# Attention maps turned by VectorE and a way through DRAM, and the products from z to the b branch in one fixed order

## The chip, the cores and the metric

The kernel runs on one core of a Trainium2 chip. The core has five engines with a queue of instructions each: TensorE (PE; its weight loads are shown apart as PEld) multiplies matrices into PSUM, VectorE (DVE) and ScalarE (ACT) work on rows of SBUF and PSUM, GpSimd (POOL) works on SBUF and issues DMAs, SyncE (SP) issues DMAs. An engine takes its instructions in the order of its queue; one that has to wait holds up everything behind it on that engine. Engines wait for one another through semaphores.

The metric is device microseconds (us) of one execution, lower is better. The kernel before takes 750.28 us, the median of 3 runs (750.06 to 750.52).

## The reference: what is computed

The program is an encoder of two layers over 256 tokens of 1024 features, all in float32. Each layer normalises its input, multiplies it by one wide matrix (`w_in`), and feeds two branches, which are gated, projected and added:

```
proj = h @ w_in[l]
(q_a, k_a, v_a, ab_a, z_a, q_b, k_b, v_b, z_b,
 gate_a, gate_b) = jnp.split(proj, SPLIT_IDX, axis=-1)
y_a = gated_delta_branch(q_a, k_a, v_a, ab_a, z_a, ...)
y_b = diff_attention_branch(q_b, k_b, v_b, z_b, cos, sin, ...)
merged = (jax.nn.sigmoid(gate_a) * (y_a @ w_pa[l])
          + jax.nn.sigmoid(gate_b) * (y_b @ w_pb[l]))
x = x + merged @ w_out[l]
```

The b branch is differential attention with 8 heads: of each head two softmax maps over 256 keys are made, one is taken from the other, and the difference is multiplied by the head's values:

```
s = jnp.einsum('nbhqd,nbhkd->nbhqk', q_blk, k)
p = jax.nn.softmax(s, axis=-1)
a = p[0] - lam * p[1]
return jnp.einsum('bhqk,bhkd->bhqd', a, v)
```

The a branch is a gated delta rule over chunks. Its triangular solve is done here by substitution within blocks of 32 tokens (on DVE), whose results are then merged on TensorE to 64 and 128.

## The kernel before

Tokens lie on the partitions in two tiles of 128. A projection of 512 columns (`proj_tm`) walks the 1024 features in eight steps of 128; a step has six products of 512 columns, for the two token tiles times three terms, since each float32 operand is split into a high and a low part (ACT casts the high part, L308, DVE subtracts for the low part, L310). A weight chunk of 512 KB, loaded by SP, serves two steps. The steps from the projections `zb` (two), `za` (two), `gb` (two), `ga` (two) to `pb` (two) are numbered 0 to 79 in what follows: step 8 is the first of the second `zb` projection, step 32 the first of `gb`.

Between these products lie the small ones of attention and of the delta rule. For a head h:

- `scores` (L1053) makes four products `sc` on TensorE, then on DVE two row maxima `mx` (L1069), on ACT four exponentials into `es` (L1071) with their sums, and on DVE the factor `cc` (L1074, L1075) and the difference of the two maps, in `es[:, 0]` (L1077, two instructions).
- `turn` (L1081) turns the map with four TensorE transposes into the PSUM tile `at` (L1088) and copies it with ACT to SBUF, tile `aT` (L1090): keys on the partitions.
- `attend` (L1093) multiplies: `av`, four products of 128x128 (L1099; each is two instructions in the trace), with `aT` as the weights that are loaded into TensorE. ACT copies `av` out and sums squares.

In the kernel before, `place(n)` names the last product of step n, and `behind(...)` makes a small product come after that one in TensorE's queue. This is a lower bound. Within it a list scheduler of the framework, which goes by priorities and by its own estimate of when operands are ready, decides the place of each instruction in every queue, and it also moves the products of a projection against one another.

Beside this, DVE runs the 31 rounds of the substitution (L870, L871, tiles `fstmp` and `X`) from the q/k projections of attention to the end of `za`, and the transposes by 32x32 blocks of the delta rule's values (`turn_squares`, L135). Their blocks go through DRAM and back to land in their new places (`bounce`: one issue on POOL out, tile `bnc_v`, L140, and four issues back, tile `tb_v`, L142). After the last round, `spread_blocks` copies `X` turned into `lt` (L874) and issues four DMAs to DRAM on POOL (`udr`, L878). `merges` reads them back: `T` (L905, four issues; those of the second group on SP) and `U` (L909, four issues). The gated attention output goes the same way through DRAM (`send`, `fetch`: `bny_yb`, L251, and `zb`, L257).

Of the kernel before, what the change touches and what calls it, by code (L numbers as in the profile page):

```python
# [8 lines left out]
F32 = mybir.dt.float32  # L9
# [40 lines left out]
def hybrid_encoder(  # L50
# [53 lines left out]
    mark = {}  # L104
# [53 lines left out]
    def norm_row(w_row, nm):  # L158
# [14 lines left out]
        for i in range(3):  # L173
            mm = T.matmul(wb[i > 0], one if i else tri[:, 0, :], hl[:, i - 1] if i else row,
                          start=i < 2, stop=i != 1)
            tc.keep_in_program_order(mm)
# [138 lines left out]
    def proj_tm(act, w, c0, n, evac, nm, places=(None,) * 4, spare=(), later=None, turned=(), between=None,  # L315
                banks=None, held=None, first=(), raws={}):

        accs = (banks or banks2)(f"pp_{nm}")
        for kt, hi, lo in weights(w, c0, n, nm, places, later=later, spare=spare, turned=turned, held=held,
                                  first=first, raws=raws):  # L320
            for m in range(NM):
                ts_ = slice(m * P, (m + 1) * P)
                o = accs[m][:, :n]
                T.matmul(o, act[kt // 4][:, 0, kt % 4, ts_], hi, start=kt == 0, stop=False)  # L324
                T.matmul(o, act[kt // 4][:, 0, kt % 4, ts_], lo, start=False, stop=False)  # L325
                mark["proj"] = T.matmul(o, act[kt // 4][:, 1, kt % 4, ts_], hi, start=False,  # L326
                                        stop=kt == KT - 1).ins
                mark["done", nm, kt] = mark["proj"]
        if between:
            between()  # L330
        for m in range(NM):
            evac(m, accs[m][:, :n])
# [76 lines left out]
    for _ in range(5):  # L409
        mm = T.matmul(idle[:, :P], ones, ones, start=True, stop=True)  # L410
        tc.keep_in_program_order(mm)
# [22 lines left out]
    for m in range(NM):  # L434
        mm = T.matmul(pos_p[:, m : m + 1], pos_r[:, m * P : (m + 1) * P], ones[0:1, 0:1], start=True, stop=True)
        mark["pos"] = mm.ins
        tc.keep_in_program_order(mm)
# [69 lines left out]
    for l in range(DEPTH):  # L507
# [86 lines left out]
        def qk_part(s_, i):  # L594
                def evac_qk(m, ps):
# [11 lines left out]
                    for b in range(4):  # L607
# [4 lines left out]
                proj_tm(hT, wl, (C_QB, C_KB)[s_] + 512 * i, 512, evac_qk, f"qk{l}{s_}{i}",  # L612
                        turned=(0, 1) if (s_, i) == (0, 1) else ())
# [170 lines left out]
        def gram(nm, g, c, slot, after=None):  # L784
            gp = (bank if slot else bank_c)(f"{nm}{l}{g}{c}")
            for j4 in range(4):
                kqh = kq[:, 4 * g + j4, c]
                with behind(after):
                    mark[nm, g, c] = T.matmul(gp[:, j4 * P : (j4 + 1) * P], kqh[:, 0, :], kqh[:, slot, :],
                                              start=True, stop=True).ins  # L790
# [35 lines left out]
        def weigh_q(g, c, after):  # L826
            bv = B[:, c, 4 * g : 4 * g + 4]
            with tc.high_priority(offset=HP):
                gp = gram("kq", g, c, 1, after)
# [67 lines left out]
        def merges(g):  # L897
# [18 lines left out]
            order = [(c, j4, mm, d) for c, j4 in every for mm in range(2) for d in range(2)]  # L916
            order.sort(key=lambda k: k != (0, 0, 1, 1))
            first = mark["pin"]
            for n_, (c, j4, mm, d) in enumerate(order):
                b0, b1 = srcdst(d, mm)  # L920
                co = 32 * (b0 % 2)
                with behind(first):
                    mm_ = T.matmul(y64p[blk(b1), c, j4, :], A[blk(b0), g, c, j4, blk(b1)],
                                   T64[blk(b0), tix(d, c, j4), co : co + 32], start=True, stop=True)
                if n_ == 0:
                    first = mm_.ins
            S.copy(y64, y64p)
            yield
            first = mark["pin"]
            zt64 = v4(bank_c(f"zt64{l}{g}")[:, :256])  # L930
            z64 = v4(bank_c(f"z64{l}{g}")[:, :256])
            for c, j4 in every:
                for mm in range(2):
                    for d in range(2):
                        b0, b1 = srcdst(d, mm)
                        with behind(first):
                            T.matmul(zt64[blk(b0), c, j4, :], y64[blk(b1), c, j4, :],
                                     U[blk(b1), tix(d, c, j4), blk(b1)], start=True, stop=True)
            for c, j4 in every:
                for d in range(2):  # L940
                    b0, b1 = srcdst(d, d)
                    T.matmul(z64[blk(b1), c, j4, :], U[blk(b1), tix(d, c, j4), blk(b1)],
                             y64[blk(b1), c, j4, :], start=True, stop=True)
            for d in range(2):
                td = slice(8 * d, 8 * d + 8)
                fl = lambda z, b: z[blk(b)].rearrange("p c h i -> p (c h) i")
                for mm in range(2):
                    b0, b1 = srcdst(d, mm)
# [7 lines left out]
            for c, j4 in every:  # L956
                for d in range(2):
                    ha, hb = halves[d], halves[1 - d]
                    with behind(mark["pin"]):
                        T.matmul(y128p[hb, c, j4, :], A[ha, g, c, j4, hb], T64[ha, tix(d, c, j4), :],  # L960
                                 start=True, stop=True)
# [3 lines left out]
            for c, j4 in every:  # L965
                for d in range(2):
                    ha, hb = halves[d], halves[1 - d]
                    with behind(mark["pin"]):
                        T.matmul(zt128[ha, c, j4, :], y128[hb, c, j4, :], U[hb, tix(d, c, j4), hb],
                                 start=True, stop=True)  # L970
# [5 lines left out]
        def chunks(g):  # L976
# [5 lines left out]
            def four(nm, lhs, rhs):  # L982
                ps = (bank if g else bank_c)(f"{nm}{l}{g}")
                for j4 in range(4):
                    with behind(mark["pin"]):
                        T.matmul(ps[:, j4 * P : (j4 + 1) * P], lhs(j4), rhs(j4), start=True, stop=True)
# [32 lines left out]
            for c in range(NM):  # L1019
                po = (bank if g else bank_c)(f"po{l}{g}{c}")  # L1020
                for j4 in range(4):
                    for d in range(2):
                        yy = y1[d] if d == c else y2[d]
                        with behind(mark["pin"]):
                            T.matmul(po[:, j4 * P : (j4 + 1) * P], B[:, c, h0 + j4, d, :], yy[:, j4, :],
                                     start=d == 0, stop=d == 1)
# [26 lines left out]
        def scores(h, after):  # L1053
# [3 lines left out]
            for qt in range(NM):  # L1057
                for n in (1, 0):
                    rows = slice(64 * n, 64 * n + 64)
                    with behind(None if qt or not n else after), tc.high_priority(offset=HP):  # L1060
                        mm = T.matmul(sp[n][:, qt * SEQ : (qt + 1) * SEQ],  # L1061
                                      qkT[h // 4][rows, 0, h % 4, qt * P : (qt + 1) * P],
                                      qkT[h // 4][rows, 1, h % 4, :], start=True, stop=True)
                    mark["sc", h] = mm.ins
                    if qt or not n:
                        tc.keep_in_program_order(mm)
# [14 lines left out]
        def turn(h, es, at):  # L1081
            with tc.high_priority(offset=HP):
                ap_ = bank(f"at{l}{h}")
                aT = work.tile([P, NM, SEQ], F32, tag="w2a", name=f"aT{l}{h}", bufs=2)
                for qt in range(NM):
                    for kt in range(NM):
                        with behind(at):
                            mark["at", h] = T.transpose(ap_[:, kt * SEQ + qt * P : kt * SEQ + (qt + 1) * P],  # L1088
                                                        es[:, 0, qt, kt * P : (kt + 1) * P], ident).ins
                S.copy(aT.rearrange("p k q -> p (k q)"), ap_)  # L1090
            return aT

        def attend(h, aT, after):  # L1093
            with tc.high_priority(offset=HP):
                op_ = bank(f"av{l}{h}")
                for qt in range(NM):
                    for kt in range(NM):
                        with behind(after):
                            T.matmul(op_[:, qt * P : (qt + 1) * P], aT[:, kt, qt * P : (qt + 1) * P],  # L1099
# [284 lines left out]
```

## Time and profile before

| what | value |
|---|---|
| median of 3 runs | 750.28 us (750.06 to 750.52) |
| span of the profiled execution, first to last instruction | 748.5 us |
| what lies around the span, by the median | 1.8 us |
| PE busy | 739.3 us, 99% of the span |
| DVE busy | 586.5 us, 78% |
| ACT busy | 481.2 us, 64% |
| POOL busy | 139.5 us, 19% |
| DMA | 135.46 MB, mean 181 GB/s |
| granted TensorE clock, mean | 0.998 |

The profiled execution is known by its span alone; its own time is that span and the 1.8 us that the runs have around it.

Each row of a profile names a line of the kernel, an engine, an operation and the tiles as out<-in. In a group's row `x128 | 18.2, 274` means 128 instructions, 18.2 us in which at least one of them ran, and 274 ns as the mean length of one. Matmuls overlap one another, so what one costs is read from the starts in the timeline, not from its length. A row of the timeline begins with its start and its length in us, and may merge several instructions (x8).

### The profile page before, as it was taken

The numbers are of one execution on the slowest core, as the hardware profiler recorded it, in microseconds if no ns is written. First come the engines' busy times: TensorE is split into PE (matmuls) and PEld (weight loads), VectorE is DVE, ScalarE is ACT, GpSimd is POOL, SyncE is SP. The second block draws the span as 40 slices with busy tenths as digits, with TensorE's granted clock in tenths as the row PEclk, the third lists the DMA queues.
The fourth block names the chain that finished last, engine by engine and source line by source line (L and its number), as shares of the span: only waits on it lengthen the run. The fifth ranks groups of instructions, "written<-read, shape, count | busy, mean of one in ns | idle before, by whom it ended". The sixth has DMA issues, their size and how long they took to land.

```text
span 748.5 us, 13917 instructions
## 1 busy us (share of the span) xinstructions
PE 739.3 (99%) x5176; PEld 641.7 (86%) x5176; DVE 586.5 (78%) x1109; ACT 481.2 (64%) x1022; POOL 139.5 (19%) x221
## 2 busy tenths in 40 slices
PE   8999999999999999999999999999999999999996
PEld 6999889987888889888889899889778888998885
DVE  8696898999985965578668779999999679537782
ACT  6757875667876576645456578555687757566552
POOL 6004110112023440100000150202110425301000
PEclk9999999999999999999999999999999999999999
DMA  8754566776667462567674466767666748335641
GB/s 260 239 170 169 170 179 198 209 211 193 208 177 186 145 184 84 171 200 247 199 232 133 128 192 180 219 176 230 195 171 195 197 133 229 95 114 201 220 141 57
DMA packets 73734, 135.46 MB, mean 181 GB/s; under 512 B 12944, under 2 KB 13921, under 8 KB 73666
## 3 DMA queue, kind: packets, MB, share of 16 engines
q1 hardware_dynamic: 64750, 113.65, 50.6%
q0 software_dynamic: 7936, 19.35, 8.7%
q10 hardware_dynamic: 980, 1.58, 0.6%
q8 instruction: 41, 0.67, 0.4%
q14 instruction: 27, 0.22, 0.1%
HBM read 125.53 MB, written 9.01 MB: 180 GB/s over the span
## 4 chain that ended last, share of the span: by engine, by line
PE 95%; ACT 2%; issue 1%; DVE 1%; DMA 1%; SPq 0%; POOLq 0%; POOL 0%; DVEq 0%; ACTq 0%
PE pp_vb L369 4%; PE pp_qk L325 4%; PE pp_qk L326 3%; PE pp_qk L324 3%; PE sc L1061 2%; PE pp_o L369 2%; PE pf_k L385 2%; PE pp_za L325 2%; PE pf_v L385 2%; PE pf_v L389 2%; PE pp_gb L324 2%; PE pp_gb L325 2%; PE pp_zb L324 2%; PE pf_q L387 2%; PE pf_k L387 2%; PE pf_v L387 2%
## 5 line engine op out<-in xcount | busy, mean ns | idle before, releaser
L325 PE MATMUL pp_qk<-lo_qk,hT 128*128 128x512 f32 x128 | 50.5, 395 | 0.3
L326 PE MATMUL pp_qk<-hi_qk,hT 128*128 128x512 f32 x128 | 50.0, 390 | 0.0
L310 DVE TENSOR_TENSOR lo_qk<-raw_qk,hi_qk 128x1024 fp32r<-128x1024 f32 x32 | 39.1, 1222 | 11.6 <-ACT hi_qk L308 11.4
L324 PE MATMUL pp_qk<-hi_qk,hT 128*128 128x512 f32 x128 | 45.1, 393 | 0.0
L308 ACT CAST hi_qk<-raw_qk 128x1024 fp32r<-128x1024 f32 x28 | 29.4, 1049 | 23.4 <-PE pp_qk L326 12.4
L1071 ACT ACTIVATE es<-sc,mx 128x256 f32<-128x256 f32 x64 | 29.6, 474 | 19.5 <-DVE mx L1069 19.5
L387 PE MATMUL pf_q<-hT,hi_q 128*128 128x256 f32 x128 | 36.1, 286 | 0.0
L385 PE MATMUL pf_k<-hT,hi_k 128*128 128x256 f32 x128 | 36.1, 287 | 0.0
L385 PE MATMUL pf_v<-hT,hi_v 128*128 128x256 f32 x128 | 35.9, 285 | 0.0
L387 PE MATMUL pf_v<-hT,hi_v 128*128 128x256 f32 x128 | 35.8, 284 | 0.0
L385 PE MATMUL pf_q<-hT,hi_q 128*128 128x256 f32 x128 | 35.8, 284 | 0.0
L387 PE MATMUL pf_k<-hT,hi_k 128*128 128x256 f32 x128 | 35.8, 284 | 0.0
L310 DVE TENSOR_TENSOR lo_pb<-raw_pb,hi_pb 128x1024 fp32r<-128x1024 f32 x16 | 19.6, 1225 | 20.5 <-ACT hi_pb L308 20.2
L389 PE MATMUL pf_q<-hT,lo_q 128*128 128x256 f32 x128 | 35.2, 288 | 0.0
L389 PE MATMUL pf_v<-hT,lo_v 128*128 128x256 f32 x128 | 34.6, 288 | 0.0
L389 PE MATMUL pf_k<-hT,lo_k 128*128 128x256 f32 x128 | 34.3, 284 | 0.0
L308 ACT CAST hi_pa<-raw_pa 128x1024 fp32r<-128x1024 f32 x16 | 16.8, 1053 | 22.3 <-PE pp_pa L326 16.1
L679 DVE SCALAR_TENSOR_TENSOR cvq<-pf_q,cw,cvq 128x254 f32<-128x254 f32 (+1 forms) x64 | 30.0, 479 | 0.9 <-ACT cvq L675 0.3
L679 DVE SCALAR_TENSOR_TENSOR cvv<-pf_v,cw,cvv 128x254 f32<-128x254 f32 (+1 forms) x64 | 30.1, 482 | 0.1
L679 DVE SCALAR_TENSOR_TENSOR cvk<-pf_k,cw,cvk 128x254 f32<-128x254 f32 (+1 forms) x64 | 29.0, 478 | 1.3 <-ACT cvk L675 0.6
L325 PEld LDWEIGHTS pp_qk<-lo_qk,hT 128*128 128x128 f32 x128 | 24.0, 188 | 6.6 <-DVE lo_qk L310 1.6
L310 DVE TENSOR_TENSOR lo_pa<-raw_pa,hi_pa 128x1024 fp32r<-128x1024 f32 x16 | 19.6, 1224 | 11.1 <-ACT hi_pa L308 11.1
(414 smaller groups left out, 2542.2 us busy)
## 6 DMA issues: line engine op xcount, KB each, us to landing
raw_qk<-in_w_in_dram SPq DMA_DIRECT2D x32, 512.0 KB, 3.8
raw_k<-in_w_in_dram SPq DMA_DIRECT2D x16, 512.0 KB, 4.7
raw_q<-in_w_in_dram SPq DMA_DIRECT2D x16, 512.0 KB, 3.7
raw_v<-in_w_in_dram SPq DMA_DIRECT2D x16, 512.0 KB, 3.8
raw_zb<-in_w_in_dram SPq DMA_DIRECT2D x16, 512.0 KB, 3.7
raw_za<-in_w_in_dram SPq DMA_DIRECT2D x16, 512.0 KB, 3.7
raw_ga<-in_w_in_dram SPq DMA_DIRECT2D x16, 512.0 KB, 4.4
raw_pb<-in_w_pb_dram SPq DMA_DIRECT2D x16, 512.0 KB, 3.8
```

The lines of the kernel that those rows point to most:

```text
L308: high = (V.tensor_copy if kp in turned else S.copy)(hi[:, :, :n], raw[:, :, :n]).ins
L310: mark[nm, kp] = high, V.tensor_tensor(lo[:, :, :n], raw[:, :, :n], hi[:, :, :n].bitcast(F32), ALU.subtract).ins
L324: T.matmul(o, act[kt // 4][:, 0, kt % 4, ts_], hi, start=kt == 0, stop=False)
L325: T.matmul(o, act[kt // 4][:, 0, kt % 4, ts_], lo, start=False, stop=False)
L326: mark["proj"] = T.matmul(o, act[kt // 4][:, 1, kt % 4, ts_], hi, start=False, stop=kt == KT - 1).ins
L369: mark["proj"] = T.matmul(o, act[kt // 4][:, pa, kt % 4, ts_], ws[kt][1 + pw], start=kt == 0 and n_ == 0, stop=kt == KT - 1 and n_ == 2).ins
L385: T.matmul(o, hi[:, cs], act[kt // 4][:, 0, kt % 4, :], start=first, stop=False, skip_group_check=True)
L387: T.matmul(o, hi[:, cs], act[kt // 4][:, 1, kt % 4, :], start=False, stop=False, skip_group_check=True)
L389: T.matmul(o, lo[:, cs], act[kt // 4][:, 0, kt % 4, :], start=False, stop=done, skip_group_check=True)
L679: V.scalar_tensor_tensor(ca[:, o0:o1], acc[:, b, o0 + sft : o1 + sft], cw[:, j, cb : cb + 1], ca[:, o0:o1], ALU.mult, ALU.add)
L1061: mm = T.matmul(sp[n][:, qt * SEQ : (qt + 1) * SEQ], qkT[h // 4][rows, 0, h % 4, qt * P : (qt + 1) * P], qkT[h // 4][rows, 1, h % 4, :], s ...
L1071: S.activation(es[:, n, qt, :], spv[:, qt, :], AF.Exp, bias=mx[:, n, qt : qt + 1], accum_out=s_all[:, h, n, qt : qt + 1])
```

## The change

**A head's map is turned on another way.** `turn` no longer uses TensorE, PSUM and ACT. DVE transposes the map by blocks of 32x32 from `es[:, 0]` into `es[:, 1]`, four key and query blocks interleaved (elements that belong together lie four apart). One DMA, issued by POOL, takes the 256 KB to DRAM (tile `att`), four more bring them back so that every block lies on its partitions (tile `aT`, two buffers). `attend` loads the weights for `av` straight from there, with a step of four elements (16 bytes) from one column to the next.

**One order.** From the first `zb` step to the end of `pb` every product goes through a new helper `mm`, which puts each behind the one issued before it. `proj_tm` becomes a generator that stops after every step; `drive` runs the steps and calls the jobs that `plan` put at a step: scores at steps 3, 7, 12, 15, 19, 23, 27 and 31, `attend` at 12, 16, 21, 24, 28, 32, 36 and 40, the delta rule's jobs at the numbers that were its lower bounds before. A job's products come after those of its step. The place of a small product is thus no longer a lower bound.

```diff
-    mark = {}
+    mark = {"chain": None}
+    def mm(*args, **kw):
+        if mark["chain"] is None:
+            return T.matmul(*args, **kw)
+        with behind(mark["chain"]):
+            made = T.matmul(*args, **kw)
+        mark["chain"] = made.ins
+        return made
...
-        def turn(h, es, at):
-            with tc.high_priority(offset=HP):
-                ap_ = bank(f"at{l}{h}")
-                aT = work.tile([P, NM, SEQ], F32, tag="w2a", name=f"aT{l}{h}", bufs=2)
-                for qt in range(NM):
-                    for kt in range(NM):
-                        with behind(at):
-                            mark["at", h] = T.transpose(ap_[:, kt * SEQ + qt * P : kt * SEQ + (qt + 1) * P],
-                                                        es[:, 0, qt, kt * P : (kt + 1) * P], ident).ins
-                S.copy(aT.rearrange("p k q -> p (k q)"), ap_)
-            return aT
+        def turn(h, es):
+            V.transpose(es[:, 1].rearrange("p q k -> p (q k)").rearrange("p (b t x) -> p b x t", b=4, x=4),
+                        es[:, 0].rearrange("p q k -> p (q k)").rearrange("p (x b t) -> p b x t", b=4, x=4))
+            dd = dram.tile([4, 32, 4, P], F32, tag="att", name=f"att{l}{h}", bufs=4)
+            G.dma_start(out=dd.rearrange("i t j x -> (i t) (j x)"), in_=es[:, 1].rearrange("p q k -> p (q k)"))
+            back = work.tile([P, 4, 32, 4], F32, tag="w2a", name=f"aT{l}{h}", bufs=2)
+            for j in range(4):
+                G.dma_start(out=back[blk(j)].rearrange("t i x k -> t i (x k)"),
+                            in_=dd[:, :, j].rearrange("i t x -> t i x"))
+            aT[h] = back
+        def attend(h):
+            op_ = bank(f"av{l}{h}")
+            av = aT[h].rearrange("p i t x -> p x (i t)")
+            for qt in range(NM):
+                for kt in range(NM):
+                    mm(op_[:, qt * P : (qt + 1) * P], av[:, 2 * qt + kt],
+                       vb[h // 4][:, kt, h % 4 * P : h % 4 * P + P],
+                       start=kt == 0, stop=kt == NM - 1)
...
+        def attention(h):
+            turn(h, scores(h))
+        def drive(gens, first):
+            for n, gen in enumerate(gens):
+                for kt in range(KT):
+                    next(gen)
+                    for job in jobs.get(KT * (first + n) + kt, ()):
+                        job()
...
+        for h in range(NH):
+            plan((3, 7, 12, 15, 19, 23, 27, 31)[h], attention, h)
+        for h in range(NH):
+            plan((12, 16, 21, 24, 28, 32, 36, 40)[h], attend, h)
```

How the queues change is shown at three places of the first layer; the second layer has the same order. First TensorE, second `zb` projection (`zb` accumulates in two PSUM tiles), around the first head's product with its values. Before:

```order
L324 MATMUL pp_zb_2172<-hi_zb_2191,hT_0_126 128x512
L1088 MATMUL at_2144<-ident,es_2106 128x128 x4
L325 MATMUL pp_zb_2171<-lo_zb_2192,hT_0_126 128x512
...
L324 MATMUL pp_zb_2171<-hi_zb_2209,hT_1_127 128x512
L324 MATMUL pp_zb_2172<-hi_zb_2209,hT_1_127 128x512
L1099 MATMUL av_2151<-vb_0_132,aT_2145 128x128 x4
L325 MATMUL pp_zb_2171<-lo_zb_2210,hT_1_127 128x512
```

And now:

```order
L110 MATMUL pp_zb_2173<-hi_zb_2210,hT_1_127 128x512
L110 MATMUL sc_2225<-qkT_0_313 128x256
L110 MATMUL sc_2224<-qkT_0_313 128x256
L110 MATMUL sc_2225<-qkT_0_313 128x256
L110 MATMUL sc_2224<-qkT_0_313 128x256
L110 MATMUL av_2249<-vb_0_132,aT_2088 128x128 x4
L110 MATMUL pp_zb_2172<-hi_zb_2210,hT_1_127 128x512
```

The four transposes `at` are gone, and the first head's `av` has moved behind the third head's scores, at the end of step 12; the products of steps 13 and on stand behind it.

Second, DVE of the changed kernel, from the first head's difference of maps (`es_2066`) to its block transpose; `X` and `fstmp` are the substitution, `thv` and `tb_v` the delta rule's values:

```order
L1071 SCALAR_TENSOR_TENSOR es_2066<-es_2066,cc_2080 128x256 x2
L321 TENSOR_TENSOR lo_zb_2193<-raw_zb_2194,hi_zb_2192 128x1024
L1063 TENSOR_REDUCE mx_2134<-sc_2136 128x2
L410 SCALAR_TENSOR_TENSOR zb_0_385<-zb_0_385,pp_zb_2029 128x512
L1063 TENSOR_REDUCE mx_2134<-sc_2135 128x2
L879 TENSOR_TENSOR X_377<-X_377,fstmp_378 128x15x17
L700 SCALAR_TENSOR_TENSOR thv_1893<-thv_1893,cvv_1896 128x256
L1079 STREAM_TRANSPOSE es_2066<-es_2066 128x4x4x32
```

Up to the transpose DVE's queue is the same as before; the transpose is a new row there, six rows behind the difference.

Third, POOL, from the substitution's end to the last two heads' maps. Before:

```order
L878 DMA udr_374<-X_377 8x8x1024 x2
L878 DMA udr_374<-lt_376 8x8x1024 x2
L909 DMA U__96<-udr_374 32x32x32 x4
L901 MEMSET T_2654 32x8x32
L902 MEMSET T_2654 32x8x32
L905 DMA T_2654<-udr_374 32x16x32 x4
```

And now:

```order
L886 DMA udr_374<-X_377 8x8x1024 x2
L886 DMA udr_374<-lt_376 8x8x1024 x2
L1082 DMA att_2554<-es_2534 128x512
L909 MEMSET T_2653 32x8x32
L910 MEMSET T_2653 32x8x32
L913 DMA T_2653<-udr_374 32x16x32 x4
L909 MEMSET T_2660 32x8x32
L910 MEMSET T_2660 32x8x32
L917 DMA U__96<-udr_374 32x32x32 x4
L1082 DMA att_2629<-es_2609 128x512
L1085 DMA aT_2556<-att_2554 32x4x128 x4
L1085 DMA aT_2631<-att_2629 32x4x128 x4
```

The seventh head's way to DRAM (`att_2554`) is issued behind the four `udr` issues, and its way back (`aT_2556`) behind the delta rule's reads `T` and `U` and behind the eighth head's way out.

234 lines of the change are left out of this document (102 added, 132 removed).

## The prediction

> **What bounds the kernel now.** I read the page first: busy times, then the chain of waits, then the granted clock by stretches.
>
> ```profile
> span 748.5 us, 13917 instructions
> PE 739.3 (99%) x5176; PEld 641.7 (86%) x5176; DVE 586.5 (78%) x1109; ACT 481.2 (64%) x1022; POOL 139.5 (19%) x221
> PE 95%; ACT 2%; issue 1%; DVE 1%; DMA 1%; SPq 0%; POOLq 0%; POOL 0%; DVEq 0%; ACTq 0%
> ```
>
> ```profile
> core 0: us, PE busy (x) PEld busy (x) DVE busy (x) ACT busy (x) POOL busy (x), PEclk, DMA share, GB/s
> 150.00:200.00 50.00, 50.00 (x254) 39.97 (x253) 48.34 (x104) 37.49 (x96) 8.07 (x15) 1.00 0.69 206
> 500.00:550.00 50.00, 50.00 (x288) 42.22 (x287) 48.83 (x110) 34.13 (x72) 8.82 (x16) 1.00 0.70 205
> ```
>
> TensorE sets the end: 99% busy, 95% of the chain. Whatever is taken from its queue shortens the span, and whatever makes it wait lengthens it, microsecond for microsecond. The second thing to see is that the change lands where VectorE has nothing to spare: 48.3 and 48.8 us busy of 50 in the stretches that hold the first heads of both layers. The new block transposes go there.
>
> **What is removed.**
>
> ```profile
> 176.95 0.60 PE L1088 MATMUL at<-ident,es 128*128 128x128 f32 x4
> 177.30 0.48 PE L325 MATMUL pp_zb<-lo_zb,hT 128*128 128x512 f32 x1
> 177.62 0.39 PE L326 MATMUL pp_zb<-hi_zb,hT 128*128 128x512 f32 x1
> 180.14 1.05 PE L1099 MATMUL av<-vb,aT 128*128 128x128 f32 x8
> 180.95 0.48 PE L325 MATMUL pp_zb<-lo_zb,hT 128*128 128x512 f32 x1
> L1088 PE MATMUL at<-ident,es 128*128 128x128 f32 x64 | 10.5, 272 | 0.0
> L1099 PE MATMUL av<-vb,aT 128*128 128x128 f32 x128 | 18.2, 274 | 0.0
> ```
>
> By starts, a head's four transposes take 177.30 - 176.95 = 0.35 us, and the product behind them 0.32, where an undisturbed one takes 0.227 (a sixth of the step worked out below): 0.35 + 0.09 = 0.44 us a head, 16 heads, **-7.0 us**. ScalarE's copies of `at` go too, but ScalarE is not on the path.
>
> **The first head of a layer.** When does TensorE reach `av`, and when is the map back?
>
> ```profile
> 159.39 0.61 PE L324 MATMUL pp_zb<-hi_zb,hT 128*128 128x512 f32 x2
> 164.97 1.14 PE L1061 MATMUL sc<-qkT 64*128 64x256 f32 x8
> 172.59 1.14 PE L1061 MATMUL sc<-qkT 64*128 64x256 f32 x8
> 173.65 0.50 PE L324 MATMUL pp_zb<-hi_zb,hT 128*128 128x512 f32 x1
> 174.56 0.89 DVE L1077 SCALAR_TENSOR_TENSOR es<-es,cc 128x256 f32<-128x256 f32 x2
> 178.95 1.24 DVE L310 TENSOR_TENSOR lo_zb<-raw_zb,hi_zb 128x1024 fp32r<-128x1024 f32 x1
> L249 DVE STREAM_TRANSPOSE zb<-ob 128x512 f32<-128x512 f32 x8 | 8.4, 1092 | 0.1
> 166.92 0.56 POOL L140 DMA_DIRECT2D bnc_v<-tb_v  x1 [11.61 <-DVE fstmp L870]
> 170.90 2.17 POOL L142 DMA_DIRECT2D tb_v<-bnc_v  x4 [3.42 <-DMA bnc_v<-tb_v]
> DMA to landing us min/median/max: 2.1/3.3/5.7
> ```
>
> Steps 0 to 3 lie between 159.39 and 164.97; less 0.1 us of entry into the scores, a step costs 5.48 / 4 = 1.37 us. The scores of head 1 (step 7) begin at 172.59 and take 1.06 + 0.11. Then follow steps 8 to 12 and head 2's scores: 172.59 + 1.17 + 5 x 1.37 + 1.16 = 181.8 is when TensorE stands at `av` of head 0.
>
> The map's way: on VectorE the new transpose takes the place just behind `thv`, where `lo_zb` starts now, 178.95, since the queue ahead of it is unchanged. With 1.09 us (the transpose of the same size and interleaving, L249) it ends at 180.0. The issue out begins some 0.3 us later, 180.3. For the delta rule's values, 256 KB by the same way, the reads begin 170.90 - 166.92 = 3.98 us behind the issue out; the last of the four starts 3 x 2.17 / 4 = 1.63 later, and lands by the last line (the landing times of `tb_v`) in 2.1 to 5.7, median 3.3; I take 3.2. 180.3 + 4.0 + 1.6 + 3.2 = 189.1. **The wait is 189.1 - 181.8 = 7.3 us**, 6.2 to 9.8 by the landing. It hits every product, since those of steps 13 and on stand behind `av`; that is the price of the fixed order. Before, `av` was taken when its operands were there. The second layer has the same queue, so twice: **+14.6**.
>
> **The seventh head.** On POOL its reads `aT` stand behind the delta rule's round through DRAM.
>
> ```profile
> 210.20 1.28 DVE L1069 TENSOR_REDUCE mx<-sc 128x2 f32<-128x512 f32 x2
> 212.54 1.10 DVE L874 COPY lt<-X 128x1024 f32<-128x1024 f32 x1
> 214.31 1.10 POOL L878 DMA_DIRECT2D udr<-lt  x2
> 222.79 3.15 POOL L909 DMA_DIRECT2D U__96<-udr  x4 [7.37 <-issue]
> 225.92 0.34 POOL L901 MEMSET T<- 32x256 f32 x1
> 226.57 2.57 POOL L905 DMA_DIRECT2D T<-udr  x4
> 580.27 1.10 POOL L878 DMA_DIRECT2D udr<-lt  x2
> 590.22 3.15 POOL L909 DMA_DIRECT2D U__96<-udr  x4 [8.85 <-issue]
> ```
>
> The chain, counted from the end of head 6's scores: two maxima and the last rounds of the substitution to the end of `lt` (210.20 to 213.6 today, behind the scores of the head before; that head's factor waits for its exponentials, so I count 3.8), 0.3 to the issue of `lt`, then 222.79 - 214.31 = 8.48 until its blocks can be read back (layer 2: 9.95). The four `T` reads now stand before `U`; I take them to run while the last of `lt` is under way, as the wait marked "issue" is 7.37 us long; if not, 2.57 more. Then two memsets 0.65, the `U` issues 3.15, `att` of the eighth head 0.56, and the same 1.63 + 3.2 to the last landing: 3.8 + 0.3 + 8.48 + 0.65 + 3.15 + 0.56 + 1.63 + 3.2 = 21.8 us; 23.2 in layer 2. TensorE has in that time nine steps (28 to 36), 12.3, one head's scores, 1.27 (1.06 with 0.1 before and 0.11 behind), and two `av`, 0.81 + 0.09 each: 15.4 us. Wait 6.4 and 7.8, if VectorE serves head 6 at once; with VectorE saturated it may be 2 late, or the backlog is gone because TensorE just waited. Bounds 4 to 13 (with late DMA landing and the `T` reads); I take **7, twice: +14**. Head 7's reads come right behind, its `av` four steps later: covered.
>
> **The other heads.** Between a head's scores and its `av` lie nine steps and one or two heads' small products, 12.3 + 3.3 to 4.3 = 15.6 to 16.6 us. The way costs some 16 to 17.5 us: from the end of `sc` of head 1 (173.76) to the end of the transpose, by today's queue, 7 to 8.5, and 0.3 + 4.0 + 1.6 + 3.2 = 9.1 behind it. Margin about nothing; each microsecond of an earlier wait lets VectorE and the DMAs catch up for those behind. 0 to 2 a layer, I take 1: **+2**.
>
> **The clock after a wait.**
>
> ```profile
> 1.11 2.50 PE L410 MATMUL idle<-ones 128*128 128x128 f32 x10 [1.11 <-DVE ones L407]
> 740.21 1.60 PE L359 MATMUL pp_o<-wB_o,mT 128*128 128x256 f32 x12
> 742.00:744.00 2.00, 0.00 (x0) 0.00 (x0) 0.75 (x4) 0.83 (x3) 0.56 (x1) 1.00 0.01 4
> 744.00:748.00 4.00, 0.00 (x0) 0.00 (x0) 0.42 (x2) 0.59 (x2) 0.00 (x0) 0.76 0.40 131
> ```
>
> TensorE's last product ends at 741.8; the granted clock is 1.00 until 744 and 0.76 on the mean of 744 to 748. From 1.00 to half speed that is a drop at 746.1, 4.3 us into the idle time. In the start, ten instructions of 128 columns take 2.50 us, 0.25 each, against 0.101 for `av` (below): a cold TensorE is slow. So each of the four waits of 7 us probably costs something after it, bounds 0 and about 2 us (4 us at half speed). I take 1 each: **+4**. [...]
>
> **The weights of `av`.** They are read at a step of 16 bytes now.
>
> ```profile
> L263 ACT ACTIVATE ybT<-zb,nw 128x512 fp32r<-128x512 f32 x8 | 9.9, 1241 | 0.0
> L244 ACT ACTIVATE yaT<-pt_ya,nw 128x512 fp32r<-128x512 f32 x8 | 5.1, 682 | 0.0
> L265 DVE SCALAR_TENSOR_TENSOR ybT<-zb,nw,ybT 128x512 fp32r<-128x512 f32 x8 | 9.2, 1146 | 0.0
> L245 DVE SCALAR_TENSOR_TENSOR yaT<-pt_ya,nw,yaT 128x512 fp32r<-128x512 f32 x8 | 5.6, 744 | 0.0
> ```
>
> Eight `av` instructions take 180.95 - 180.14 = 0.81 us by starts, 0.101 each, while 128 columns at the rate of a long product (0.227 for 512) would take 0.057: the weight load paces them, so a dearer load is not hidden. No load in the trace reads at such a step. The nearest rows are ScalarE's and VectorE's, where `zb` is read in this interleaving and `pt_ya` is not: 0.56 and 0.40 us more for 512 columns, 0.14 and 0.10 for 128. With 128 loads (x128 above): 13 to 18 us if TensorE pays the same, 0 if its load does not mind. I take **+8**, between them, as no row is from TensorE itself. [...]
>
> **Off the path.** 16 transposes on VectorE (16 x 1.09 = 17.5 us), 80 issues on POOL (80 x 0.55 = 44 us, beside 139.5 busy) and 8 MB of DMA: hidden by TensorE's 739 us except where they make the waits above longer. If VectorE's part were not hidden in the first stretches, its 1.1 us a head would come on top, some 4 us a layer; this lies within the bounds of the other heads' term.
>
> **Sum.** 748.5 - 7 + 14.6 + 14 + 2 + 4 + 8 = 784.1. The runs have 1.8 us around the profiled span (750.28 - 748.5): **786 us**.
>
> **Rivals.**
>
> - *Dear weights.* TensorE pays what ScalarE's row shows: 18 in place of 8, 796 us. For it: the load paces `av`. Against: no such load has a row. [...]
> - *Only the first head waits.* The framework's queue stays as it is, but the DMA ways are shorter there (landing 2.1) or VectorE ahead, since TensorE has just stood still; the seventh head's 7 fall to 0 to 1, and two clock returns with them: 786 - 14 - 2 - 2 (the other heads) - 4 (cheap weights) = 764 us. For it: the backlog on VectorE works off at each wait. Against: 8.48 us of the seventh head's chain is DMA that stands so in the trace.
> - *The map comes home in time* (the other side). Nothing waits and the weights cost nothing, so only the -7.0 is left: 750.3 - 7 = 743.3. It is decided at the first `av`: the map must have landed by 181.8, 7.3 us earlier than I count. For it: VectorE's queue between the difference of the maps (174.56 today) and the transpose holds 4.4 us of other work, which may be done earlier where VectorE is ahead. Against: the smallest landing (2.1) gives 1.1, and the 3.98 between issue out and reads is a measured way, not a guess; even both together leave some 2 us.
> - *It cancels*: waits shorter by half, cheap weights, sum zero: 750 us.
>
> **How the numbers follow.** Forecast 0.64, 786 us, own range 766 (weights 0, waits at their low bounds) to 804 (weights 18, waits and clock near the high ones). Dear weights 0.09, only the first head 0.14, home in time 0.10, cancels 0.03. A measurement of this kernel tells 0.2%, 1.5 us, from no change. So faster 0.10, same 0.03, slower 0.87. The range of 8 in 10 leaves out the last two cases (0.13) and the far ends of the forecast's: 757 to 802.
>
> **What would show it.** TensorE idle before `av` of the first head, ended by a DMA into `aT`, about 7 us, and again before the seventh head's; POOL's `aT` reads of head 6 behind `U`; the granted clock below 1.00 behind those gaps; starts of `av` more than 0.101 us apart. Starts at 0.101 refute the weight term; a gap of under 4 us at head 0 refutes the way's price; no gap at head 6 with `aT` issued late refutes the POOL chain. The forecast is wrong as a whole if TensorE stays above 98% busy.

## The result, and the profile after

The changed kernel takes **793.3 us** (median of 4 runs, 792.7 to 794.4) against 750.2 us of the kernel before beside it: a ratio of 1.0573, 95% interval 1.0558 to 1.0588. It is slower by 43 us. The forecast was 786 us, 757 to 802.

The page of the changed kernel, its first lines, the chain of waits and the group of `av`:

```profile
span 792.7 us, 13972 instructions
PE 754.0 (95%) x5112; PEld 651.8 (82%) x5112; DVE 602.6 (76%) x1125; ACT 475.2 (60%) x1006; POOL 183.6 (23%) x301
...
PE 83%; DMA 4%; POOL 3%; DVE 3%; ACT 3%; issue 3%; POOLq 0%; DVEq 0%; ACTq 0%
...
L110 PE MATMUL av<-vb,aT 128*128 128x128 f32 x128 | 31.7, 399 | 26.4 <-DMA aT<-att 26.4
```

TensorE's share falls from 99% to 95%, and in the chain from 95% to 83%: it now stands and waits. The group of `av` shows two things in one line. 26.4 us of idle time before it end with a DMA into `aT`, and one `av` instruction takes 399 ns in the mean where it took 274 before. Next TensorE's waits by what ended them (us in total, times, longest):

```profile
PE av L110 <- DMA aT<-att: 26.4, 4, 7.8
PE pp_zb L110 <- DVE lo_zb L321: 2.6, 2, 1.3
...
PE pp_gb L110 <- DVE lo_gb L321: 0.8, 2, 0.4
```

Four waits for a map, two a layer. The timeline of TensorE shows where they are in the first layer (and the first one of the second), with the way of the first map on VectorE and POOL below it:

```profile
181.36 0.50 PE L110 MATMUL pp_zb<-lo_zb,hT 128*128 128x512 f32 x1 [1.32 <-DVE lo_zb L321]
182.71 1.13 PE L110 MATMUL sc<-qkT 64*128 64x256 f32 x8
189.49 2.21 PE L110 MATMUL av<-vb,aT 128*128 128x128 f32 x8 [5.65 <-DMA aT<-att]
196.97 1.13 PE L110 MATMUL sc<-qkT 64*128 64x256 f32 x8
225.38 1.90 PE L110 MATMUL av<-vb,aT 128*128 128x128 f32 x8
249.75 2.21 PE L110 MATMUL av<-vb,aT 128*128 128x128 f32 x8 [7.79 <-DMA aT<-att]
578.63 2.21 PE L110 MATMUL av<-vb,aT 128*128 128x128 f32 x8 [5.76 <-DMA aT<-att]
586.07 1.13 PE L110 MATMUL sc<-qkT 64*128 64x256 f32 x8
```

```profile
179.14 1.10 DVE L1079 STREAM_TRANSPOSE es<-es 128x512 f32<-128x512 f32 x1
180.07 1.23 DVE L321 TENSOR_TENSOR lo_zb<-raw_zb,hi_zb 128x1024 fp32r<-128x1024 f32 x1
```

```profile
180.80 0.56 POOL L1082 DMA_DIRECT2D att<-es  x1 [7.53 <-ACT es L1065]
...
183.87 2.19 POOL L1085 DMA_DIRECT2D aT<-att  x4 [0.72 <-PE sc L110]
```

The first map's way is the forecast one: transpose at 179.1, out at 180.8, reads from 183.9, `av` at 189.5. TensorE came to `av` at 183.8, 2 us later than forecast, for the most part since it had just waited 1.3 us for `lo_zb`, which VectorE did behind the new transpose. An undisturbed head's `av` takes 1.90 us in the timeline (225.38) against 1.05 before. Last, the granted clock in the stretches around the first and the seventh head's wait:

```profile
core 0: us, PE busy (x) PEld busy (x) DVE busy (x) ACT busy (x) POOL busy (x), PEclk, DMA share, GB/s
184.00:186.00 2.00, 0.00 (x0) 0.00 (x0) 2.00 (x6) 0.36 (x1) 2.00 (x4) 1.00 1.00 357
186.00:188.00 2.00, 0.00 (x0) 0.00 (x0) 2.00 (x5) 1.59 (x8) 1.52 (x4) 0.83 0.91 284
190.00:192.00 2.00, 2.00 (x10) 1.90 (x9) 0.42 (x1) 0.27 (x1) 0.56 (x1) 0.50 0.34 131
192.00:194.00 2.00, 2.00 (x6) 1.57 (x5) 0.00 (x0) 0.91 (x5) 1.73 (x4) 0.50 0.44 164
194.00:196.00 2.00, 2.00 (x10) 1.59 (x9) 0.63 (x1) 1.05 (x1) 2.00 (x4) 0.96 0.43 117
252.00:254.00 2.00, 2.00 (x6) 1.51 (x6) 0.00 (x0) 1.17 (x5) 0.00 (x0) 0.50 0.66 118
254.00:256.00 2.00, 2.00 (x7) 1.56 (x6) 0.37 (x1) 1.45 (x2) 0.00 (x0) 0.60 0.00 0
```

TensorE is busy from 189.5 on, but at half clock until 194.2 (0.96 in the stretch from 194). In stretches of 0.2 us the clock reads 1.00 up to 187.2, 0.85 in the next and 0.50 from 187.4: the drop came at 187.3, 3.5 us after TensorE's last product. Behind the seventh head's wait the half clock lasts to 255.6 (0.50 in the 0.2 us before, 0.98 in those after).

### The profile page after: what moved, and what is told of

The parts are those of the page before. It is cut to its first block, busy times and chain, and to the rows that moved or that the text cites. A ratio compares the mean times of both kernels' runs of the same rounds, so it can differ in the third digit from the quotient of the medians.

```text
span 792.7 us, 13972 instructions
## 1 busy us (share of the span) xinstructions
PE 754.0 (95%) x5112; PEld 651.8 (82%) x5112; DVE 602.6 (76%) x1125; ACT 475.2 (60%) x1006; POOL 183.6 (23%) x301
## 4 chain that ended last, share of the span: by engine, by line
PE 83%; DMA 4%; POOL 3%; DVE 3%; ACT 3%; issue 3%; POOLq 0%; DVEq 0%; ACTq 0%
PE pp_qk L108 10%; PE pp_zb L110 6%; PE pp_ga L110 6%; PE pp_pb L110 6%; PE pp_pa L108 6%; PE pp_gb L110 4%; PE pp_vb L380 4%; PE pp_o L108 3%; PE av L110 2%; PE pp_o L380 2%; PE pf_k L396 2%; PE pf_v L396 2%; PE pf_v L400 2%; PE pf_q L398 2%; PE pf_k L398 2%
## 5 line engine op out<-in xcount | busy, mean ns | idle before, releaser
L110 PE MATMUL av<-vb,aT 128*128 128x128 f32 x128 | 31.7, 399 | 26.4 <-DMA aT<-att 26.4
L108 PEld LDWEIGHTS pp_qk<-hi_qk,hT 128*128 128x128 f32 x256 | 47.4, 188 | 9.1
L110 PEld LDWEIGHTS av<-vb,aT 128*128 128x128 f32 x128 | 31.1, 325 | 28.5 <-issue 28.0
L110 PE MATMUL pp_ga<-hi_ga,hT 128*128 128x512 f32 x128 | 45.6, 407 | 0.0
L110 PE MATMUL pp_za<-hi_za,hT 128*128 128x512 f32 x128 | 43.7, 402 | 0.0
L110 PE MATMUL pp_zb<-hi_zb,hT 128*128 128x512 f32 x128 | 43.5, 412 | 0.0
L110 PE MATMUL pp_pb<-hi_pb,ybT 128*128 128x512 f32 x128 | 42.7, 399 | 0.0
L1085 POOL DMA_DIRECT2D aT<-att x64 | 36.1, 570 | 22.1 <-DMA att<-es 18.9
L110 PE MATMUL pp_gb<-hi_gb,hT 128*128 128x512 f32 x112 | 40.8, 424 | 0.0
L108 PE MATMUL pp_pa<-hi_pa,yaT 128*128 128x512 f32 x128 | 39.8, 389 | 0.0
```

Source lines behind the costliest of these rows:

```text
L108: return T.matmul(*args, **kw)
L110: made = T.matmul(*args, **kw)
L1085: G.dma_start(out=back[blk(j)].rearrange("t i x k -> t i (x k)"), in_=dd[:, :, j].rearrange("i t x -> t i x"))
```

## The experiments

The theory: the 43 us are four waits for maps (26.4), dearer weights of `av`, the slow clock behind the waits, and a little VectorE, less the transposes saved. Each has a rival: that the fixed order itself costs the time, that the weights are dear only beside the DMAs, that the waits merely show a VectorE or DMA that is the bound anyhow.

### The fixed order alone (e1_order_alone)

```diff
-            V.transpose(es[:, 1] ..., es[:, 0] ...)      # and the five DMAs
+            for qt in range(NM):
+                for kt in range(NM):
+                    with behind(mark["chain"]):
+                        mark["chain"] = T.transpose(...).ins
+            S.copy(aT[h].rearrange("p k q -> p (k q)"), ap_)
...
+        for h in range(NH):   # turn two steps ahead of attend
+            jobs.setdefault((10, 14, 18, 22, 26, 30, 34, 38)[h], []).insert(0, lambda h=h: turn(h))
```

> The fixed order with the old turning: TensorE transposes each map (two steps ahead of its product with the values) and ScalarE copies it, everything else as in the changed kernel. Theory: the fixed order by itself costs nothing, since what it pins is ready in time; 750 us, within 2. Rival: the order itself holds TensorE up, because a product whose low part or scores are late now stops all behind it; 754 to 762 us.

Measured: 751.4 us, ratio 1.0012 (1.0002 to 1.0022), 0.9 us more than before. The list of waits has none of TensorE in these stretches. The fixed order is not the cause; a place in it becomes a wait only if its operand is late.

### The step of the weights alone (e2_step16_alone, e2_step8_alone)

The kernel before, with its own order and transposes; only the copy to SBUF puts neighbours 16 bytes apart, and in the second run 8:

```diff
-                S.copy(aT.rearrange("p k q -> p (k q)"), ap_)
+                S.copy(aT.rearrange("p q (t k) -> p k t q", k=NM), ap_.rearrange("p (k t q) -> p k t q", ...))
...
-                            T.matmul(..., aT[:, kt, qt * P : (qt + 1) * P],
+                            T.matmul(..., aT[:, :, 2 * qt + kt],
```

> The kernel before, with its own order and its TensorE transposes; only ScalarE's copy writes the map with four elements between neighbours, so that the weights of av are loaded at a step of 16 bytes. Theory: the load of 128 columns at that step takes 0.33 us and is not hidden: 1.0 us a head, 16 us in all, 766 us (764 to 768). Rival: the load was dear in the changed kernel only for the lower clock behind its waits or the DMAs beside it; 750 to 753 us.

> The kernel before, weights of av at a step of 8 bytes (two elements) instead of 16. [...] If it goes with the step as such: half of the 13.5 us of the step of 16, 756 to 758 us; if any step costs the same, 763 us.

Measured: 763.8 us at 16 bytes, ratio 1.0186 (1.0169 to 1.0203), so 14.0 us more, just under the theory's 764 to 768; 751.1 us at 8 bytes, ratio 1.0015 (1.0006 to 1.0025), 1.1 us more. The weight loads by tile: before, at 16 bytes, at 8 bytes (ns min/median/max).

```profile
L1099 PEld LDWEIGHTS av<-vb,aT x128: 187/192/193, 179.9 to 605.5; 128*128 128x128 f32 x128
```

```profile
L1099 PEld LDWEIGHTS av<-vb,aT x128: 308/329/332, 179.7 to 618.9; 128*128 128x128 f32 x128
```

```profile
L1099 PEld LDWEIGHTS av<-vb,aT x128: 193/196/198, 180.3 to 606.9; 128*128 128x128 f32 x128
```

The step of 16 bytes makes a load 137 ns longer, in a kernel where TensorE waits for nothing in these stretches and the granted clock is 0.998, as in the kernel before. It costs 14 us by itself, and half that step costs almost nothing. (128 loads of 137 ns more would be 17.5 us; by starts eight `av` instructions take 1.71 us in place of 0.81, so 0.11 us of each load shows and the rest is hidden. ScalarE's copy gets dearer too, 489.0 us busy in place of 481.2, but no product waits for it.) The 14 us are twice what the transposes cost by the prediction's estimate: 0.88 us a head against 0.44. With this layout the change could not win even if no map were ever late.

### Weights that lie side by side (e3_contig)

```diff
-            dd = dram.tile([4, 32, 4, P], F32, tag="att", name=f"att{l}{h}", bufs=4)
-            G.dma_start(out=dd.rearrange("i t j x -> (i t) (j x)"), in_=...)
+            dd = dram.tile([32, 16, 4, 32], F32, tag="att", name=f"att{l}{h}", bufs=4)
+            for i in range(4):
+                G.dma_start(out=dd[:, :, i], in_=es[blk(i), 1] ...)
...
-            for j in range(4):
-                G.dma_start(out=back[blk(j)] ..., in_=dd[:, :, j] ...)
+            G.dma_start(out=back ..., in_=dd.rearrange("t (j x) i k -> j t (x i k)", j=4))
```

> The changed kernel with weights that lie side by side: the map goes out in four DMAs of pieces of 128 bytes and comes back in one, so av loads without a step. Theory: av falls back to 0.11 us a product, 1.0 us a head less, 16 us; the waits for the map stay and may grow or shrink by 2 us each with the other DMAs; 770 to 785 us. Rival, the step of the weights is not the cause: 790 us or more.

Measured: 823.1 us, ratio 1.0975 (1.0958 to 1.0992), 30 us slower than the change instead of 16 faster. The time lies in the rival's range, but not for the rival's reason; that is in the waits:

```profile
PE av L110 <- DMA aT<-att: 58.2, 8, 9.0
```

```profile
L110 PEld LDWEIGHTS av<-vb,aT x128: 187/240/338, 192.3 to 676.4; 128*128 128x128 f32 x128
```

Eight waits instead of four, 58.2 us instead of 26.4. The loads did get cheaper where nothing waits: 192 ns in the eight heads without a wait, as before the change, and some 333 in the eight behind a wait, at half clock (in the mean of the run the granted clock is 0.958, against 0.978 in the changed kernel); the median lies between them. But the way is longer. The first map's four issues out begin at 180.40, the one read back only at 186.85, and `av` starts at 192.30 (189.49 in the changed kernel). POOL's order adds to it: the third head's four issues out stand from 193.02 to 195.5, but its read stands behind the next head's issues, which wait until 207.53, and begins at 210.84; its `av` waits 8.85 us.

### The products with the values later (e5_later)

```diff
-            plan((12, 16, 21, 24, 28, 32, 36, 40)[h], attend, h)
+            plan((18, 22, 26, 29, 33, 37, 43, 46)[h], attend, h)
```

> The changed kernel with av of the eight heads at steps 18, 22, 26, 29, 33, 37, 43 and 46 instead of 12, 16, 21, 24, 28, 32, 36 and 40. Theory: the maps are home by then, so the four waits for them (26.4 us) and the slow clock behind them (about 6 us) go; 758 to 764 us, with the dear weights (16 us) left. Rival: VectorE and the DMAs are the bound of these stretches, and the time lost only moves to other waits; 775 us or more.

Measured: 770.6 us, ratio 1.0270 (1.0255 to 1.0286): 22.7 us less than the change, where the theory had 29 to 35. TensorE's waits in this run:

```profile
PE pp_ga L110 <- DVE lo_ga L321: 3.0, 2, 1.5
PE sc L110 <- ACT es L1065: 2.8, 4, 1.2
PE pp_zb L110 <- DVE lo_zb L321: 2.6, 2, 1.3
```

No product waits for a map any more: the four waits were a matter of place. Of the 32 us that the theory counted (26.4 and 6) some 10 did not come. 5.8 us of them are waits that the standing still had hidden or that the places made, for `lo_ga` and for scores behind late exponentials; a wait of 0.6 for `lo_za` is new too, and the rest is not taken apart. The time lies between the two ranges: the rival is right for these waits, not for the other 22.7 us.

### VectorE's transposes alone (e9_dve)

The fixed order with TensorE's transposes, and beside them the new block transposes into a place that nobody reads:

```diff
+            V.transpose(es[:, 1] ..., es[:, 0] ...)
             return es
```

> The fixed order with TensorE's transposes (751.4 us), and beside them VectorE's block transposes of the changed kernel, whose result nobody reads. It asks what the transposes cost where VectorE is full. Theory: 1.1 us more on VectorE ahead of the second zb projection's low parts holds up TensorE at one place of each layer, as the changed kernel shows (1.3 us before a product with lo_zb): 753 to 755 us. Rival: VectorE has the room, nothing waits: 751 us. Other rival: every one of the first heads' transposes counts, 4 us a layer: 759 us.

Measured: 757.4 us, ratio 1.0099 (1.0084 to 1.0114), against 1.0012 without them: 0.87% or 6.5 us, between the theory and the second rival and within neither. TensorE's waits:

```profile
PE pp_za L110 <- DVE lo_za L321: 1.7, 2, 0.9
PE pp_zb L110 <- DVE lo_zb L321: 1.6, 2, 0.8
...
PE pp_gb L110 <- DVE lo_gb L321: 0.7, 2, 0.3
```

Three places a layer where a low part is late. These waits come to 4.0 us; TensorE's busy time is 2.5 us longer beside them (743.0 us, 740.5 in e1). A product of 512 columns is 0.39 us long, but the next starts 0.227 after it, so part of a late start lies inside that length and no wait shows it. The 17.8 us of transposes are hidden for about two thirds only. This leaves next to nothing of the 7.0 us that TensorE saves by the prediction's estimate, whatever the way through DRAM costs.

### The seventh head's reads ahead of the delta rule's (e6_pool)

```diff
+            with behind(mark["aT6"]):    # the memsets, T's and U's reads on POOL
+                ...
+            with behind(mark["aT6"] if h == 7 else None):   # the eighth head's way out
```

> The changed kernel with POOL's queue mended: the reads aT of the seventh head stand ahead of the delta rule's T and U (they follow the seventh map's own way out), the eighth head's way out behind them. Theory: the seventh head's map is home some 4 to 5 us earlier, its wait falls from 7.7 to 3 in both layers, and with so short an idle stretch the clock does not drop there (3.4 us for both layers): 793 - 9 - 3 = 781 us (778 to 785). Rival: the landing of att behind the udr transfers (8.5 us) is what holds it, not the place on POOL, or U becomes late for the merge in its turn: 788 us or more.

Measured: 791.4 us, ratio 1.0544 (1.0522 to 1.0565): 2 us less, a sixth of what was expected, within the rival and hardly clear of the change's own interval (1.0558 to 1.0588). POOL's queue in the changed kernel, and in this run:

```profile
229.40 1.16 POOL L886 DMA_DIRECT2D udr<-X  x2
230.53 1.10 POOL L886 DMA_DIRECT2D udr<-lt  x2
231.63 0.60 POOL L1082 DMA_DIRECT2D att<-es  x1
...
241.47 3.12 POOL L917 DMA_DIRECT2D U__96<-udr  x4
245.14 0.57 POOL L1082 DMA_DIRECT2D att<-es  x1 [0.55 <-DMA T<-udr]
245.70 2.17 POOL L1085 DMA_DIRECT2D aT<-att  x4
```

```profile
231.32 0.60 POOL L1086 DMA_DIRECT2D att<-es  x1
239.07 2.20 POOL L1089 DMA_DIRECT2D aT<-att  x4 [7.15 <-issue]
...
248.81 2.19 POOL L1089 DMA_DIRECT2D aT<-att  x4
```

And TensorE's waits in it, with one of them and the granted clock behind it:

```profile
PE av L110 <- DMA aT<-att: 21.6, 6, 6.9
```

```profile
243.07 2.10 PE L110 MATMUL av<-vb,aT 128*128 128x128 f32 x8 [1.41 <-DMA aT<-att]
```

```profile
244.00:246.00 2.00, 2.00 (x9) 1.78 (x9) 0.00 (x0) 0.75 (x3) 1.91 (x5) 0.83 0.39 102
246.00:248.00 2.00, 2.00 (x6) 1.60 (x5) 0.00 (x0) 0.89 (x4) 2.00 (x3) 0.50 0.65 133
```

The reads did move from 245.7 to 239.1, and the seventh head's waits shrank from 7.8 and 7.2 us to 1.4 and 3.1. But the reads still begin 7.7 us behind the way out, and the eighth head's reads, now behind `T` and `U`, start at 248.8: its `av` waits 1.7 and 3.3 us, and there are six waits now instead of four. The place on POOL was one cause of the seventh head's wait; of the 10.5 us that it cost, half comes back at the eighth head.

The waits fall by 4.8 us in all, the time by 2. Most of the difference is the clock: it drops behind all six waits, also behind the one of 1.4 us, where it reads 0.83 from 244 to 246 and 0.50 from 246 to 248, by estimate a drop at 245.3, more than 2 us after TensorE has begun to work again (243.07). By estimate (half of the working time at half clock behind `av`, read from narrow stretches) the drops cost 7.8 us in this run, where the same estimate gives 5.6 in the changed kernel.

### The clock behind the waits (e4_warm, e4_warm0)

```diff
             op_ = bank(f"av{l}{h}")
+            for _ in range({0: 11, 6: 16}.get(h, 0)):     # e4_warm0: {0: 10}
+                mm(op_[:, :SEQ], ident, ..., start=True, stop=True)
```

> The changed kernel, with idle products of 256 columns (of the identity, into av's own PSUM tile, overwritten afterwards) in TensorE's queue ahead of av of the first head (11) and of the seventh (16): about 2.9 and 4.2 us of work inside the waits of 5.7 and 7.8 us. Theory: the waits stay as long as they are, since the maps come when they come, but the idle stretches are under 4 us and the granted clock stays at 1.00; what the half speed behind the four waits cost, 6 us, comes back: 787 us (785 to 789). Rival: the slow products behind the waits are slow for another cause (DMA, SBUF), or the drop costs nothing on the path: 792 to 795 us.

Measured: 799.5 us, ratio 1.0656 (1.0635 to 1.0677), slower than the change and outside both ranges. The filling was sized wrong: a product of 256 columns took two instructions of 0.23 us, so eleven took 5.0 us and sixteen 7.3. Beside that a new wait for `hi_gb` came up ahead of the seventh head, 3.1 us in the first layer and 3.6 in the second, and the clock fell in the first all the same (0.89 from 240 to 244, 0.69 from 244 to 248). As a whole the run decides nothing; its first head does, and the next run repeats that alone.

> The changed kernel with ten idle products of 256 columns ahead of av of the first head alone, 4.5 us at the 0.23 us of an instruction that the run before with such products showed, inside waits of 5.7 and 5.9 us. Theory: the map comes when it comes, the clock stays at 1.00 in both places, and the stretch behind gets shorter by what it got shorter in that run's first layer, 1.35 us, so 793.3 - 2.7 = 790.6 us (789.5 to 791.5). Rival: the drop costs nothing on the path, 793.3.

Measured: 791.3 us, ratio 1.0530 (1.0512 to 1.0549). The difference to 1.0573 is in the expected direction, but the runs spread over 3 us, so the trace says more than the time:

```profile
185.27 4.58 PE L110 MATMUL av<-qkT,ident 128*128 128x256 f32 x20
190.51 2.11 PE L110 MATMUL av<-vb,aT 128*128 128x128 f32 x8 [0.66 <-DMA aT<-att]
196.64 1.13 PE L110 MATMUL sc<-qkT 64*128 64x256 f32 x8
```

The granted clock of the same run, in the columns of the stretches above:

```profile
182.00:200.00 18.00, 16.49 (x77) 13.20 (x78) 14.72 (x29) 9.21 (x27) 10.96 (x20) 1.00 0.65 203
```

From `av` to the next scores, the same work takes 196.64 - 190.51 = 6.13 us at a clock of 1.00, and 196.97 - 189.49 = 7.48 in the changed kernel. The drop costs 1.35 us behind this wait, and 586.07 - 578.63 = 7.44 less the same 6.13, 1.3, in the second layer. It is the products behind `av` that pay: from the start of `av` to the next product it is 1.86 us in both runs, at half clock and at full.

### All repairs together (e7_all, e7_nopool)

The DMAs of e3_contig, `av` at steps 19, 24, 28, 31, 35, 39, 45 and 47, and in e7_all also POOL's order of e6_pool.

> All repairs at once: contiguous weights by the other DMAs, av at steps 19, 24, 28, 31, 35, 39, 45 and 47, the seventh head's read ahead of T and U. Theory: the parts add up, so what is left of the change are the transposes saved (-7.0), the order (+1) and VectorE's transposes (+6 as measured beside the fixed order, up to 10 with what new waits the later places gave): 750 to 756 us. Rival: the longer way of these DMAs keeps TensorE waiting even at the later places: 765 us or more.

> The run with all repairs (774.4 us), with POOL's queue again as the scheduler makes it: contiguous weights and the later places alone. Theory: the 10.4 us that the merges waited there for T came from putting the seventh head's read ahead of T; they go, and head 6's place at step 45 is late enough for its map: 762 to 767 us. Rival: T is late because of the many small pieces that go out to DRAM before it, whatever the order on POOL: 772 to 776 us.

Measured: 774.4 us with POOL's order mended, ratio 1.0317 (1.0298 to 1.0335), and 767.8 us (763.5 to 769.8) without, 1.0220 (1.0175 to 1.0266). Waits of the first, then of the second:

```profile
PE y64p L110 <- DMA T<-udr: 10.4, 2, 5.6
PE sc L110 <- ACT es L1068: 6.1, 6, 2.2
```

```profile
PE sc L110 <- ACT es L1065: 5.4, 4, 1.8
...
PE zt L110 <- DMA U__96<-udr: 1.7, 1, 1.7
```

For e7_all the rival had the time right and the cause only in part: no product waits for a map any more, but whoever goes first on POOL, the other is late, here the merge for 10.4 us. With the scheduler's order that wait goes but for some 3 us at `zt` and `z`, as the theory of e7_nopool had it; the median lies just above its range, and the runs scatter too much to settle the last 3 us. No version tried beats the kernel before. By estimate from e1 and e9 none with all sixteen maps on this way can by much: 750.2 - 7.0 + 0.9 + 6.5 is 750.6 with nothing else late and no dear weight.

## Why the prediction was right, and where its steps were off

Side, mechanisms and range were right; the time was 7 us too low, and errors of both signs hid in it: -5.2 us for the first and the other heads, +12.6 for the rest, 6.0 of it for the weights.

| step | forecast | shown |
|---|---|---|
| transposes saved | -7.0 | not run alone; e1 keeps them |
| the order by itself | 0 | +0.9 (e1) |
| first head, both layers | +14.6 | +11.4 (5.65 and 5.76) |
| seventh head, both layers | +14 | +15.0 (26.4 less the two above) |
| other heads | +2 | 0 |
| low parts late (VectorE) | 0 | +3.4 (2.6 and 0.8) |
| clock | +4 | +5.3: 2.65 by e4_warm0, 2.65 by starts |
| weights of `av` | +8 | +14.0 (e2) |
| sum from 750.2 | 786 | 793.2; measured 793.3 |

That the sum comes so near to the measured time is luck in part. The -7.0 was never run alone, and for VectorE the table takes the waits in the changed kernel; with e9's 6.5 in place of 3.4 the sum is 796.

**The first head.** Transpose, issue, reads and end of the wait came within 0.5 us of the forecast times; the wait was 1.7 us shorter because TensorE itself came 2 us late. That lateness is the step "off the path", which called VectorE's part hidden: the transpose stands in front of the `lo_zb` of the coming step. The bound given for it, 4 us a layer, held.

**The seventh head.** The size is right for a wrong sum. From the end of head 6's scores (223.5) to its `av` (249.75) it took 26.2 us, not 21.8: POOL came to `udr` only behind the sixth head's reads (issue of `lt` at 230.53), and the four `T` reads did not fit into the wait for `lt`, the case priced at 2.57. TensorE's own work in that time was 18.5 us, not 15.4, through the dear `av` and a late `lo_gb`. The two errors nearly cancelled: luck.

**The weights.** This is the term that was mis-sized, and most of the miss. The rows of ScalarE and VectorE at the same step gave 13 to 18 us; 8 was chosen as the middle towards nothing, for want of a row of TensorE. The measured 14.0 lies at VectorE's row. The reason given, that the load paces `av`, was right in the main: of the 17.5 us by which the 128 loads grew, 14.0 reached the time.

**The clock.** The drop came 3.5 us after the last product, where the tail of the kernel before had it after 4.3 (1.00 from 745 to 746, 0.53 from 746 to 747). The slow start that the prediction set beside it, 0.25 us an instruction, shows no drop: the granted clock reads 1.00 there, from 0 to 6 us. The 4 us at half speed in its bound were an estimate that no row of the kernel before shows; the changed kernel shows 4.7 (189.5 to 194.2) and 5.9 (249.75 to 255.6) in the first layer. The prediction's 1 us a wait was too low for the first heads (1.35 and 1.3). Behind the seventh heads' waits the 17 products that follow `av` start over 5.85 us (251.61 to 257.46) in the first layer and over 4.72 (639.73 to 644.45) in the second, where 17 products behind an undisturbed `av` take 3.96 (227.04 to 231.00): 1.9 and 0.8 more. So a wait cost 0.8 to 1.9, 5.3 in all. That shorter waits are safe, which e4_warm and e6_pool took for granted, is not always so: in e6_pool a wait of 1.4 us was followed by half clock too (0.50 from 246 to 248).

**The rivals.** "Dear weights" (796) comes nearer to the measured 793.3 than the forecast of 786 does. Its term, 18, is 4 too high where the forecast's 8 is 6 too low, so the truth lies between the two. "Only the first head waits" is refuted by the second pair of waits, "home in time" and "it cancels" by all four waits and by e2.

## What to carry to other kernels

Price the layout of an operand as well as the work that it saves: taking 0.44 us a head of transposes off the bound engine was paid back twice by loading weights at a step of 16 bytes, while a step of 8 bytes cost 1.1 us in all. A fixed order costs next to nothing by itself (0.9 us here), but in it each of the four late maps was a wait of the whole engine (26.4 us in all), and slow products followed each of them; so give such a place the measured way of its operand plus room. Before a transfer goes onto a queue that others need, look at who stands behind it: in e6_pool half of what the mended order saved came back at the next head, and in e7_all the merge was late in place of `av`.

## What the runs showed of the hardware that was not expected

A weight load of 128 float32 columns took 192 ns at a step of 4 bytes (before), 196 at 8 (e2_step8_alone) and 329 at 16 (e2_step16_alone): 4 ns more for the first doubling and 133 for the second, so it does not go with the step. At half clock the load without a step grew to some 333 ns (e3_contig), while in the changed kernel, four of whose `av` run at half clock, no load at the step of 16 takes more than 332.

A way through DRAM had no one price here: the first head's reads began 3.1 us behind their issue out (180.80 to 183.87), the seventh head's, in the run where nothing else stood before them on POOL, 7.7 us (231.32 to 239.07), with four `udr` transfers issued just ahead.

How long TensorE stands still did not alone decide whether the clock dropped: in e6_pool it fell to 0.50 behind a wait of 1.4 us, more than 2 us after work had begun again, while in e7_nopool a wait of 1.7 us for `U` (249.94) was followed by none: 1.00 from 248 to 260. What decides it, no run here separates.
